# The feed-forward first half with tokens as the stationary operand, 512 weight columns moving, f transposed, and first tokens' products inside the second tokens' norm

## The chip, the cores and the metric

One core of one Trainium2 chip runs the whole program in one launch. The metric is device microseconds (us) of that launch, the median over the runs shown; rows of the trace come from one further, profiled execution. TensorE is called PE in the rows, its weight loads PEld, VectorE DVE, ScalarE ACT, GpSimd POOL, and SyncE, which issues most transfers, SP.

## The reference

Two decoder layers over 256 tokens of width 1024. Each layer is feed-forward, mixer (three attentions and gates), feed-forward; each of these six stages starts with an RMS norm whose scale and shift come from a vector c through the large matrix `w_ada`, and ends by adding a gated result to x.

```python
def swiglu(h, wg, wu, wd):
    return (jax.nn.silu(h @ wg) * (h @ wu)) @ wd
...
for l in range(DEPTH):
    h = pre(x, 0)
    x = x + 0.5 * mod[:, 0, 2] * swiglu(h, w_ffn_gate[l, 0], w_ffn_up[l, 0], w_ffn_down[l, 0])
    h = pre(x, 1)
    ...
    x = x + mod[:, 1, 2] * (merged @ w_out[l])
    h = pre(x, 2)
    x = x + 0.5 * mod[:, 2, 2] * swiglu(h, w_ffn_gate[l, 1], w_ffn_up[l, 1], w_ffn_down[l, 1])
return rmsnorm(x, final_gain)
```

Here `wg` and `wu` are 1024 x 2816 and `wd` is 2816 x 1024, so the inner width is 22 blocks of 128.

## The kernel before, in words

The stages are numbered s = 0 to 5: 0, 2, 3 and 5 are feed-forwards, 1 and 4 are mixers. All instructions stand in the order of the Python code; every engine works through its own queue in that order.

**Units.** Every weight matrix comes through SBUF in raws of 1 MB (three buffers). A raw is cut into units of 128 x 1024 numbers. For each unit `feed` puts a rounded copy `wH` on ScalarE (L150) and the remainder `wL` on VectorE (L158), up to five units ahead of the products, in six buffers each. The activations are split the same way (hH and hL, ffH and ffL), and a matrix product is the sum of three: hH with wH, hH with wL, hL with wH. `step` feeds, takes at most one tick of the `w_ada` work (a multiply-add `acc` on VectorE, L282, over a transfer of 512 KB), issues the unit's products, and then the elementwise work of the unit before (`post`, and a part `later` that comes one unit after it).

**First half of a feed-forward.** `aform` (L595) holds a 128 x 128 block of the weights in TensorE and lets 256 tokens of hH or hL move: 24 products per unit, one inner block fb per unit, gate and up side by side in one PSUM bank. The result stands with the inner width on the partitions, which is what the second half needs: `up_post` makes silu (ScalarE, L653), f = up times silu (VectorE, L654), and then ffH (L657) and ffL (L658).

**Second half and mixer output.** `run_rows` holds 128 x 128 blocks of ffH or ffL, with tokens as columns, and lets 512 columns of `wd` move (`bform`, L707, PSUM names pd and pe).

**From one stage to the next.** The last four units are done for tokens 0 to 127 (t = 0) first and for the second half of the tokens (t = 1) last. So the norm of t = 0 (transposes `psn` at L489, scale and shift at L506 and L508, cast to hH at L520, remainder hL at L526) runs under the last products, and the norm of t = 1 comes after them: residual, square, rsqrt on GpSimd, xn on ScalarE and VectorE, transposes, hH, hL. Three kinds of work may stand in between: `ada_reduce` sums a finished `acc` over the partitions (PE, `adag` at L343 for a gate, `adam` at L352 and L358 for scale or shift), and N1 says how many of the sums stand ahead of the second transposes; before a mixer `v_early` does the products of the first two v units (L943, PSUM pv) for t = 0. Before a feed-forward nothing of that kind is done. A mixer then loads its bias table (L440) through GpSimd's queue and further raws of `w_in` through SP's.

Of the kernel before, what the change touches and what calls it, by code (L numbers as in the profile page):

```python
# [16 lines left out]
P = 128  # L17
# [26 lines left out]

N1 = (0, 1, 2, 2, 1, 0)

# [43 lines left out]
class Trunk:  # L90
# [28 lines left out]
    def load_raws(self):  # L119
        while self.n_raw < min(self.raw_cap, len(self.raws)):  # L120
# [15 lines left out]
            self.n_raw += 1  # L136

    def feed(self, ahead=AHEAD, high=0):

        self.load_raws()  # L140
        nc = self.nc
        lim = min(self.consumed + ahead, self.consumed + NB - 1, len(self.units) - 1)
        while self.n_l <= lim:
            want_h = max(min(self.n_l + 1, lim), self.consumed + high)
            while self.n_h <= want_h:
                u = self.units[self.n_h]
                k, n = u.shape
                th = self.sp.tile([P, 1024], F32R, tag="wH", name=f"wH{self.n_h}", bufs=NB)
                u.H = th[:, : k * n].rearrange("p (k n) -> p k n", k=k)
                nc.scalar.copy(u.H, u.view(self.raw_tiles[u.raw]))  # L150
                self.n_h += 1
# [369 lines left out]

    def norm_low(self, t, h32):
        sl = slice(t * P, (t + 1) * P)
        for q in range(2):
# [45 lines left out]
    def step(self, u):  # L570
# [3 lines left out]
        self.done()  # L574
        if self.pending:
            self.pending()
            self.pending = None
        if u.post:
            self.pending = u.post()

    def flush(self):
        if self.pending:
            self.pending()
            self.pending = None

# [21 lines left out]
    def plan_ffn(self, l, i, s):  # L607
        a = self.a
        wg, wu, wd = a["w_ffn_gate"][l, i], a["w_ffn_up"][l, i], a["w_ffn_down"][l, i]
        plan = {"kind": "ffn", "s": s, "in": [], "out": []}  # L610
        ps = {}

# [23 lines left out]

        def gate_pe(fb):
            def pe(u, part="all"):
                if part != "low":
                    ps[fb] = self.ps(f"pf{s}_{fb}")  # L640
                self.aform(u, ps[fb][:, :S], self.hH, self.hL, part=part)
            return pe

        def up_pe(fb):
            return lambda u: self.aform(u, ps[fb][:, S:], self.hH, self.hL)

        def up_post(fb):
            def post():
                nc = self.nc
                p = ps[fb]  # L650
                sil = self.sil[:, fb % 3, :]
                f32 = self.f32[:, fb % 3, :]
                nc.scalar.activation(sil, p[:, :S], AF.Silu)  # L653
                nc.vector.tensor_tensor(f32, p[:, S:], sil, op=ALU.mult)  # L654

                def later():
                    nc.scalar.copy(self.ffH[:, fb, :], f32)  # L657
                    nc.vector.tensor_tensor(self.ffL[:, fb, :], f32, self.ffH[:, fb, :], op=ALU.subtract)  # L658
                return later
            return post  # L660

        if s == 0:
            plan["start"] = []
            k4 = lambda t, n: t[:, :4 * n].rearrange("p (k n) -> p k n", k=4)
            for q in range(4):
# [11 lines left out]
                plan["start"].append(us)  # L677
        for q in range(3 if s == 0 else 0, NF // 2):
            rg, ru = self.col_raw(wg, ((q * 256, 256),)), self.col_raw(wu, ((q * 256, 256),))
            for r, mk in ((rg, gate_pe), (ru, up_pe)):  # L680
                for b in range(2):
                    fb = 2 * q + b
                    view = lambda t, b=b: t.rearrange("p (k n) -> p k n", k=KB)[:, :, b * P:(b + 1) * P]
                    u = Unit(r, view, (KB, P), mk(fb), up_post(fb) if r == ru else None)
                    self.units.append(u)
                    plan["in"].append(u)
        plan["out"] = self.plan_rows(wd, NF)
# [21 lines left out]
    def run_rows(self, us, s, xh, xl, early=None):  # L709
# [4 lines left out]
        last = s == 5  # L714
        nxt = [ch for ch, at in self.filler.items() if at == s]
        cols = PIECES
# [4 lines left out]
        for kb in range(n - TAIL):  # L721
# [5 lines left out]
            self.done()  # L727
            self.flush()
        for c in LATE:
# [60 lines left out]
    def alloc_ffn(self, s):  # L790
        self.ffH = self.sp.tile([P, NF, S], F32R, tag="bigA", name=f"ffH{s}", bufs=1)
        self.ffL = self.sp.tile([P, NF, S], F32R, tag="bigB", name=f"ffL{s}", bufs=1)
        self.sil = self.sp.tile([P, 3, S], F32, tag="oA", name=f"sil{s}", bufs=1)
        self.f32 = self.sp.tile([P, 3, S], F32, tag="oB", name=f"f32{s}", bufs=1)

    def run_ffn(self, plan, early=None):
# [3 lines left out]
        if s:  # L800
            us = plan["in"][:2]
            for u in us:
                self.feed()
                self.ada_tick()
                u.pe(u, "high")
            for u in us:
                u.pe(u, "low")
            self.done(2)
        for i, u in enumerate(plan["in"]):
            if i > 1 or s == 0:  # L810
# [5 lines left out]
        self.flush()  # L816
        self.run_rows(plan["out"], s, self.ffH, self.ffL, early)
# [117 lines left out]
    def v_pe(self, i, u, pv, ts=(0, 1), part="all"):  # L935
        for t in ts:
            sl = slice(t * P, (t + 1) * P)
            out = pv[t][i // 4][:, (i // 2 % 2) * 256:(i // 2 % 2) * 256 + 256]
            seq = [(self.hH, w, k) for k in range(4) for w in (u.H, u.L)] + [(self.hL, u.H, k) for k in range(4)]
# [6 lines left out]
    def v_early(self, plan):  # L946

        s = plan["s"]
        plan["pv"] = [[self.ps(f"pv{s}_{t}_{i}") for i in range(2)] for t in range(2)]
        for i in range(2):  # L950
            self.v_pe(i, plan["v"][i], plan["pv"], (0,))

    def v_post(self, t, pv):
        self.nc.scalar.copy(self.v[:, t, 0:512], pv[0])
        self.nc.scalar.copy(self.v[:, t, 512:768], pv[1][:, 0:256])

# [181 lines left out]

    def run_mixer(self, plan):
        s, l = plan["s"], plan["l"]  # L1140
# [11 lines left out]
        pv = plan["pv"]  # L1152
        for i, u in enumerate(plan["v"]):
            self.feed()
            self.ada_tick()
            self.v_pe(i, u, pv, (1,) if i < 2 else (0, 1), "high" if i < 2 else "all")
            if i == 1:
                for k in range(2):
                    self.v_pe(k, plan["v"][k], pv, (1,), "low")
                self.done(2)  # L1160
            elif i > 1:
                self.done()
        for t in range(2):
# [25 lines left out]
        for i, u in enumerate(sum(plan["br"], [])):  # L1189
# [4 lines left out]
            for fn, arg in when.get(("br", i), ()):  # L1194
                fn(arg)
        self.flush()
        self.run_rows(plan["out"], s, self.mH, self.mL)

    def run(self):
        nc, a = self.nc, self.a  # L1200
        self.pending = None
        self.ada_setup()
# [97 lines left out]
        for n, plan in enumerate(plans):  # L1300
# [14 lines left out]
            if s == 5:  # L1315
                self.fg = self.sp.tile([P, D], F32, tag="gate", name="fg", bufs=2)
                nc.gpsimd.dma_start(self.fg, a["final_gain"].unsqueeze(0).to_broadcast([P, D]))
            if plan["kind"] == "ffn":
                mix = plans[n + 1] if n + 1 < len(plans) and plans[n + 1]["kind"] == "mix" else None
                self.run_ffn(plan, (lambda: self.v_early(mix)) if mix else None)  # L1320
            else:
                self.run_mixer(plan)

# [28 lines left out]
```

## Time and profile before

| what | value |
|---|---|
| median of 3 runs | 1208.26 us (1208.2 to 1210.25) |
| profiled execution, its own time | 1207.99 us |
| its span in the trace | 1206.3 us |
| granted TensorE clock, mean | 0.998 of full speed |
| busy share PE, DVE, ACT | 98%, 69%, 51% |

The profiled execution is 0.27 us under the median, and 1.7 us of its time lie outside the span. Busy time of PE is the union of instructions whose modelled ends overlap, so the distance from start to start, which the pieces of the chain give as time divided by count, is what one product costs.

### The profile page before, as it was taken

The page shows a single profiled execution, that of the slowest core. Times are in us where ns is not written, and L with a number is a line of the kernel's source. Part 1 is how long each engine was busy: PE and PEld are TensorE (multiplying, and loading weights), DVE is VectorE, ACT ScalarE, POOL GpSimd, SP SyncE. Part 2 cuts the span into 40 slices and gives each one's busy share as a digit, 9 for nine tenths or more (in the row PEclk, how much of TensorE's full clock was granted, in tenths as well). Part 3 has the DMA queues.
Part 4 walks back from the last instruction along what each step waited for, and adds up shares of the span by engine and source line. Part 5 has one row for each costly group of instructions (what it writes and reads, how often), then busy time and mean ns, then how long its engine had stood idle before and what let it go on. Part 6 is the DMA issues. An engine that isn't in the chain of part 4 may idle for free.

```text
span 1206.3 us, 21161 instructions
## 1 busy us (share of the span) xinstructions
PE 1177.2 (98%) x8765; PEld 1099.6 (91%) x8765; DVE 838.2 (69%) x1087; ACT 615.7 (51%) x953; POOL 37.7 (3%) x74
## 2 busy tenths in 40 slices
PE   6999999999999999999999999999999999999997
PEld 5999988899999899998889999889999998999986
DVE  3677776768788797777687676666866788555544
ACT  5555443565564574444364545345655446444432
POOL 1001000300000000000000000012000000000000
PEclk9999999999999999999999999999999999999999
DMA  9999789796658678788849777759853574656550
GB/s 317 310 312 314 268 303 321 127 334 214 209 190 313 213 248 284 264 300 278 294 142 302 265 259 255 271 159 211 292 202 114 177 276 147 204 179 195 177 184 35
DMA packets 190440, 285.35 MB, mean 237 GB/s; under 512 B 8006, under 2 KB 156780, under 8 KB 190344
## 3 DMA queue, kind: packets, MB, share of 16 engines
q1 hardware_dynamic: 187656, 279.88, 69.5%
q0 software_dynamic: 2544, 3.93, 2.6%
q8 instruction: 68, 1.11, 0.4%
q14 instruction: 28, 0.23, 0.1%
q10 hardware_dynamic: 144, 0.20, 0.0%
HBM read 282.77 MB, written 1.20 MB: 235 GB/s over the span
## 4 chain that ended last, share of the span: by engine, by line
PE 87%; DMA 3%; ACT 3%; DVE 3%; issue 2%; POOL 1%; SPq 0%; POOLq 0%; ACTq 0%; DVEq 0%
PE pf L595 39%; PE pd L707 21%; PE pg L595 12%; PE pq L595 3%; PE pb L595 3%; PE pf L625 3%; DMA raw<-in_w_in 2%; DVE wL L158 1%; ACT wH L150 1%; PE adaf L211 1%; DMA first<-in_w_ada 1%; ACT jk L453 1%; ACT h L508 1%; PE pv L943 1%; PE adag L343 0%
## 5 line engine op out<-in xcount | busy, mean ns | idle before, releaser
L158 DVE TENSOR_TENSOR wL<-raw,wH 128x1024 fp32r<-128x1024 f32 (+1 forms) x384 | 462.1, 1212 | 251.2 <-ACT wH L150 250.7
L150 ACT CAST wH<-raw 128x1024 fp32r<-128x1024 f32 (+1 forms) x384 | 394.2, 1041 | 275.5 <-PE pd L707 112.5
L595 PE MATMUL pf<-hH,wH 128*128 128x256 f32 x1312 | 323.9, 285 | 1.1 <-DVE hH L506 1.1
L595 PE MATMUL pf<-hH,wL 128*128 128x256 f32 x1312 | 322.1, 283 | 0.0
L595 PEld LDWEIGHTS pf<-hH,wH 128*128 128x128 f32 x1312 | 251.8, 192 | 4.1 <-DVE hH L506 1.8
L595 PEld LDWEIGHTS pf<-hH,wL 128*128 128x128 f32 x1312 | 252.2, 192 | 0.2 <-issue 0.2
L595 PE MATMUL pf<-hL,wH 128*128 128x256 f32 x1312 | 183.7, 283 | 0.0
L595 PEld LDWEIGHTS pf<-hL,wH 128*128 128x128 f32 x1312 | 169.1, 192 | 0.0
L282 DVE SCALAR_TENSOR_TENSOR acc<-ada,sc,acc 128x1024 f32<-128x1024 f32 x112 | 143.3, 1279 | 5.3 <-DMA ada<-in_w_ada 5.3
L707 PE MATMUL pd<-wH,ffH 128*128 128x512 f32 x336 | 131.3, 391 | 0.0
L707 PE MATMUL pd<-wL,ffH 128*128 128x512 f32 x336 | 130.9, 390 | 0.0
L707 PE MATMUL pd<-wH,ffL 128*128 128x512 f32 x336 | 130.9, 389 | 0.0
L595 PE MATMUL pg<-hH,wH 128*128 128x256 f32 x384 | 96.1, 288 | 0.0
L595 PE MATMUL pg<-hH,wL 128*128 128x256 f32 x384 | 94.0, 283 | 0.0
L653 ACT ACTIVATE sil<-pf 128x256 f32<-128x256 f32 x88 | 33.3, 382 | 108.2 <-PE pf L595 108.2
L595 PEld LDWEIGHTS pg<-hH,wH 128*128 128x128 f32 x384 | 73.4, 191 | 2.7 <-issue 0.9
L707 PEld LDWEIGHTS pd<-wH,ffH 128*128 128x128 f32 x336 | 63.1, 188 | 13.7 <-issue 0.8
L707 PEld LDWEIGHTS pd<-wH,ffL 128*128 128x128 f32 x336 | 63.1, 188 | 13.1
L707 PEld LDWEIGHTS pd<-wL,ffH 128*128 128x128 f32 x336 | 63.1, 188 | 12.8
L595 PEld LDWEIGHTS pg<-hH,wL 128*128 128x128 f32 x384 | 73.6, 192 | 0.0
L654 DVE TENSOR_TENSOR f<-pf,sil 128x256 f32<-128x256 f32 x88 | 36.9, 422 | 34.0 <-ACT sil L653 34.0
L595 PE MATMUL pq<-hH,wH 128*128 128x256 f32 x224 | 56.1, 288 | 0.0
(214 smaller groups left out, 1456.0 us busy)
## 6 DMA issues: line engine op xcount, KB each, us to landing
ada<-in_w_ada SPq DMA_DIRECT2D x128, 512.0 KB, 5.4
raw<-in_w_ffn_down SPq DMA_DIRECT2D x44, 1024.0 KB, 5.1
raw<-in_w_in SPq DMA_DIRECT2D x42, 1024.0 KB, 6.7
raw<-in_w_ffn_gate SPq DMA_DIRECT2D x41, 1024.0 KB, 5.9
raw<-in_w_ffn_up SPq DMA_DIRECT2D x41, 1024.0 KB, 5.5
first<-in_w_ada SPq DMA_DIRECT2D x32, 256.0 KB, 6.0
raw<-in_w_out SPq DMA_DIRECT2D x8, 1024.0 KB, 5.8
raw<-in_w_ffn_gate SPq DMA_DIRECT2D x12, 256.0 KB, 6.0
```

The source lines that it names most:

```text
L150: nc.scalar.copy(u.H, u.view(self.raw_tiles[u.raw]))
L158: nc.vector.tensor_tensor(u.L, u.view(self.raw_tiles[u.raw]), u.H, op=ALU.subtract)
L211: self.nc.tensor.matmul(self.first_ps[q % 2][32 * i:32 * i + 32, 0:P], w, src[:, i * P:(i + 1) * P], start=kb in (0, None), stop=kb == KB - 1)
L282: self.nc.vector.scalar_tensor_tensor(acc, src, sc, acc, ALU.mult, ALU.add)
L453: nc.scalar.activation(junk[:, :w], self.x[:, t, lo:lo + w], AF.Square, scale=1.0 / 32.0, accum_out=ms[:, n:n + 1])
L508: nc.scalar.activation(out[:, fb, :], src, AF.Identity, bias=sb, scale=sa)
L595: nc.tensor.matmul(out, w[:, kb, cs], x[:, kb, :], start=i == 0, stop=i == n - 1)
L625: self.nc.tensor.matmul(ps[fb][:, S * up:S * up + S], w[:, 2 * k + up, b * P:(b + 1) * P], x[:, 2 * q + k, :], start=q == 0 and not up and ...
L653: nc.scalar.activation(sil, p[:, :S], AF.Silu)
L654: nc.vector.tensor_tensor(f32, p[:, S:], sil, op=ALU.mult)
L707: self.nc.tensor.matmul(out, x[:, kb, sl], w[:, 0, hs], start=first and i == 0, stop=last and i == 2)
L943: self.nc.tensor.matmul(out, x[:, 4 * (i % 2) + k, sl], w[:, k, :], start=i % 2 == 0 and j == 0, stop=i % 2 == 1 and j == n - 1)
```

## The change

The first half of the feed-forward turns round: a 128 x 128 block of hH or hL (tokens as columns) is held, and 512 columns of `wg` or `wu` move (`cols_pe`). The inner width is done in groups of four blocks (and a last group of two, with 256 columns); a group has four units of gate and four of up, a unit being two k blocks by 512 columns. The result stands with tokens on the partitions, so f is transposed: `cols_post` makes f for a group, and its `later`, one unit after that, issues four transposes per token half (`pft`) and takes ffH and ffL from PSUM. In stage 0 the first six blocks keep the old form. hH and hL become two halves of one tile.

At a stage's end every next stage now has an early part (`ffn_early`, `v_early`): the products of the next stage's first units for t = 0 stand ahead of the second transposes, and one `ada_reduce` fewer does (N1). The second half of hL of t = 0 is made after xn, the third unit's wH is fed before the second transposes and its wL between hH and h32 of t = 1, and the first units' products with hL of t = 1 come last. `flush` at the end of each row loop becomes `drain`, which takes posts one unit later.

```diff
-N1 = (0, 1, 2, 2, 1, 0)
+N1 = (0, 0, 1, 1, 0, 0)
...
             evac(self.hH[:, :, sl])
             for f in between:
                 f()
+            self.feed(2)
         evac(h32)
...
-        self.hH = self.sp.tile([P, KB, S], F32R, tag="hH", name=f"hH{s}", bufs=1)
-        self.hL = self.sp.tile([P, KB, S], F32R, tag="hL", name=f"hL{s}", bufs=1)
+        self.hHL = self.sp.tile([P, KB, 2, S], F32R, tag="hHL", name=f"hHL{s}", bufs=1)
+        self.hH, self.hL = self.hHL[:, :, 0, :], self.hHL[:, :, 1, :]
...
         if u.post:
-            self.pending = u.post()
+            self.pending.append(u.post)
+
+    def drain(self):
+
+        todo, self.pending = self.pending, []
+        for f in todo:
+            later = f()
+            if callable(later):
+                self.pending.append(later)
...
+        def cols_pe(g, up, k0, nk, n):
+
+            def pe(u, ts=(0, 1), part="all"):
+                for t in ts:
+                    if k0 == 0 and part != "low":
+                        pg[g, up, t] = self.ps(f"pf{s}_{g}_{up}_{t}")
+                    out = pg[g, up, t][:, :n]
+                    sl = slice(t * P, (t + 1) * P)
+                    seq = [(self.hH, w, k) for k in range(nk) for w in (u.H, u.L)]
+                    seq += [(self.hL, u.H, k) for k in range(nk)]
+                    for i in {"all": range(3 * nk), "high": range(2 * nk), "low": range(2 * nk, 3 * nk)}[part]:
+                        x, w, k = seq[i]
+                        self.nc.tensor.matmul(out, x[:, k0 + k, sl], w[:, k, :], start=k0 == 0 and i == 0,
+                                              stop=k0 + nk == KB and i == 3 * nk - 1)
+            return pe
...
+        def cols_post(g, n):
+
+            def post():
+                nc = self.nc
+                f = wide(self.f32, n)
+                for t in range(2):
+                    nc.vector.tensor_tensor(f[:, t, :], pg[g, 1, t][:, :n], wide(self.sil, n)[:, t, :], op=ALU.mult)
+
+                def later():
+                    b = n // P
+                    for t in range(2):
+                        pt = self.ps(f"pft{s}_{g}_{t}")
+                        for i in range(b):
+                            nc.tensor.transpose(pt[:, i * P:(i + 1) * P], f[:, t, i * P:(i + 1) * P], self.ident)
+                        src = pt[:, :n].rearrange("p (b n) -> p b n", b=b)
+                        sl = slice(t * P, (t + 1) * P)
+                        H, L = self.ffH[:, g:g + b, sl], self.ffL[:, g:g + b, sl]
+                        nc.scalar.copy(H, src)
+                        nc.vector.tensor_tensor(L, src, H, op=ALU.subtract)
                 return later
             return post
...
-        if early:
-            self.norm_low(0, h0)
-            early()
+        self.norm_low(0, h0, (0,))
+        early()
         xn1 = self.norm_x(1, s + 1)
-        if not early:
-            self.norm_low(0, h0)
+        self.feed_high(self.consumed + 2)
+        self.norm_low(0, h0, (1,))
...
+            us = plan["in"][:3]
+            for u in us[:2]:
+                self.ada_tick()
+                u.pe(u, (1,), "high")
+            self.ada_tick()
+            us[2].pe(us[2], (0,))
+            us[2].pe(us[2], (1,), "high")
             for u in us:
+                u.pe(u, (1,), "low")
+                self.done()
                 self.feed()
```

How the change moves instructions is seen at three places. First TensorE's queue from the mixer's last product (pe) of stage 1 to the first products of stage 2 (pf); wH and wL are weights, psn the norm's transposes of the second tokens, adag a filler sum. Before:

```order
L707 MATMUL pe_768_4487<-wH_4452,mHL_4025 128x256
L343 MATMUL adag_0_4615<-acc_2_3915,ones 128x512
L343 MATMUL adag_1_4616<-acc_2_3915,ones 128x512
L489 MATMUL psn_1_0_4627<-ident,xn_1_4622 128x128 x4
L489 MATMUL psn_1_1_4632<-ident,xn_1_4622 128x128 x4
L595 MATMUL pf_0_4682<-hH_4574,wH_4470 128x256
```

And of the change: the twelve products of units 0 and 1 for the first tokens begin right behind the last pe, and these rows are the last three of them and what follows.

```order
L672 MATMUL pf_0_0_0_4237<-wH_4110,hHL_4196 128x512
L672 MATMUL pf_0_0_0_4237<-wL_4112,hHL_4196 128x512
L672 MATMUL pf_0_0_0_4237<-wH_4110,hHL_4196 128x512 x2
L491 MATMUL psn_1_0_4259<-ident,xn_1_4253 128x128 x4
L491 MATMUL psn_1_1_4264<-ident,xn_1_4253 128x128 x4
L345 MATMUL adag_0_4269<-acc_2_3535,ones 128x512
L345 MATMUL adag_1_4270<-acc_2_3535,ones 128x512
L672 MATMUL pf_0_0_1_4316<-wH_4092,hHL_4196 128x512
```

The first tokens' products have taken the place of the sum adag, which now stands between the second tokens' transposes and their first products. Second, TensorE's queue of the change around the transposes (pft) of stage 2's first group; the products ahead of them are those of the next group's second unit, the products behind them those of its third.

```order
L672 MATMUL pf_4_0_1_4465<-wL_4376,hHL_4196 128x512
L672 MATMUL pf_4_0_1_4465<-wH_4374,hHL_4196 128x512 x2
L698 MATMUL pft_0_0_4493<-ident,f_4315 128x128 x4
L698 MATMUL pft_0_1_4500<-ident,f_4315 128x128 x4
L672 MATMUL pf_4_0_0_4458<-wH_4396,hHL_4196 128x512
```

Two units of products (24) stand between the end of a group and its transposes. Third, VectorE's queue of the change at the same place: f is the product of up and silu, and the wL ahead of it belongs to the unit that is fed just before.

```order
L284 SCALAR_TENSOR_TENSOR acc_0_4321<-ada_4360,sc,acc_0_4321 128x1024
L160 TENSOR_TENSOR wL_4454<-raw_4351,wH_4452 128x1024
L691 TENSOR_TENSOR f_4315<-pf_0_1_0_4380,sil_4314 128x512
L691 TENSOR_TENSOR f_4315<-pf_0_1_1_4387,sil_4314 128x512
L160 TENSOR_TENSOR wL_4476<-raw_4378,wH_4474 128x1024
L284 SCALAR_TENSOR_TENSOR acc_0_4321<-ada_4401,sc,acc_0_4321 128x1024
L703 TENSOR_TENSOR ffL_4313<-pft_0_0_4493,ffH_4312 128x4x128
L703 TENSOR_TENSOR ffL_4313<-pft_0_1_4500,ffH_4312 128x4x128
```

Where four pairs of f and ffL of 256 columns stood one by one between the wL, two of 512 stand together now, and the ffL wait for transposes.

## Rows read from the trace of the kernel before

**Rows 1.** The page's head and its busy times: us, share of the span, instructions

```profile
span 1206.3 us, 21161 instructions
...
PE 1177.2 (98%) x8765; PEld 1099.6 (91%) x8765; DVE 838.2 (69%) x1087; ACT 615.7 (51%) x953; POOL 37.7 (3%) x74
```

**Rows 2.** The page's chain that ended last, by engine and line

```profile
PE pf L595 39%; PE pd L707 21%; PE pg L595 12%; PE pq L595 3%; PE pb L595 3%; PE pf L625 3%; DMA raw<-in_w_in 2%; DVE wL L158 1%; ACT wH L150 1%; PE adaf L211 1%; DMA first<-in_w_ada 1%; ACT jk L453 1%; ACT h L508 1%; PE pv L943 1%; PE adag L343 0%
```

**Rows 3.** Windows, stage 2's first half: us, busy us (count), clock, DMA share, GB/s

```profile
425.00:553.00 128.00, 128.00 (x1071) 126.89 (x1071) 98.18 (x120) 67.66 (x100) 0.00 (x0) 1.00 0.83 279
```

**Rows 4.** The chain's pieces in order of time: start us, us, what, count

```profile
60.84 48.96 PE pf L595 x408
...
318.22 0.98 PE pt_dil L1109 x9
...
806.18 1.09 PE psn L489 x8
...
808.35 1.72 PE adag L343 x4
...
1011.61 127.21 PE pf L595 x1056
...
1138.82 54.44 PE pd L707 x240
```

**Rows 5.** Groups by form: count | busy us, mean ns of one | idle before, releaser

```profile
L158 DVE TENSOR_TENSOR wL<-raw,wH 128x1024 fp32r<-128x1024 f32 x372 | 452.0, 1223 | 244.3 <-ACT wH L150 243.8
...
L150 ACT CAST wH<-raw 128x1024 fp32r<-128x1024 f32 x372 | 385.4, 1050 | 272.7 <-PE pd L707 112.5 <-PE pf L595 73.4 <-issue 29.9
...
L282 DVE SCALAR_TENSOR_TENSOR acc<-ada,sc,acc 128x1024 f32<-128x1024 f32 x112 | 143.3, 1279 | 5.3 <-DMA ada<-in_w_ada 5.3
...
L536 DVE SCALAR_TENSOR_TENSOR y<-pd,gate 128x512 f32<-128x512 f32 x24 | 16.5, 688 | 14.8 <-PE pd L707 14.8
...
L506 DVE TENSOR_SCALAR h<-psn,modv 128x128 f32<-128x128 f32 x40 | 13.6, 403 | 0.0
```

**Rows 6.** Timeline, PE, stage 1 to 2: start, us, [idle before <-releaser]

```profile
419.34 1.88 PE L343 MATMUL adag<-acc,ones 128*128 128x512 f32 x4
...
422.63 1.09 PE L489 MATMUL psn<-ident,xn 128*128 128x128 f32 x8 [1.41 <-DVE xn L478]
...
424.15 0.39 PE L595 MATMUL pf<-hH,wH 128*128 128x256 f32 x1 [0.43 <-DVE hH L506]
```

**Rows 7.** Timeline, ACT and DVE, same place

```profile
420.15 0.62 ACT L520 CAST hH<-h 128x512 fp32r<-128x512 f32 x1
...
422.09 0.49 DVE L478 TENSOR_SCALAR xn<-x,r 128x512 f32<-128x512 f32 x1 [0.66 <-POOL r L468]
```

**Rows 8.** Timeline, PE, stage 2 to 3

```profile
617.53 1.09 PE L489 MATMUL psn<-ident,xn 128*128 128x128 f32 x8 [0.85 <-DVE xn L478]
...
619.05 0.39 PE L595 MATMUL pf<-hH,wH 128*128 128x256 f32 x1 [0.21 <-DVE hH L506]
```

**Rows 9.** Timeline, PE, stage 0 to 1

```profile
218.58 0.28 PE L707 MATMUL pe<-wH,ffL 128*128 128x256 f32 x1
...
220.16 0.39 PE L943 MATMUL pv<-wH,hH 128*128 128x256 f32 x1 [1.30 <-ACT hH L520]
...
229.37 0.39 PE L943 MATMUL pv<-wL,hH 128*128 128x256 f32 x1 [0.62 <-DVE wL L158]
...
247.24 0.39 PE L595 MATMUL pq<-hH,wL 128*128 128x256 f32 x1 [0.34 <-DVE wL L158]
```

**Rows 10.** Timeline, PE, stage 3 to 4

```profile
817.67 1.36 PE L943 MATMUL pv<-wH,hL 128*128 128x256 f32 x8 [0.62 <-DVE hL L526]
...
819.75 0.39 PE L943 MATMUL pv<-wL,hH 128*128 128x256 f32 x1 [0.61 <-DVE wL L158]
```

**Rows 11.** The chain's pieces, transfers behind the two mixers' starts

```profile
230.48 14.29 DMA raw<-in_w_in
...
820.86 13.75 DMA raw<-in_w_in
```

More of the change, by code (lines that the diff above doesn't have):

```diff
@@ L136, in load_raws, with feed_high @@
             self.n_raw += 1
+    def feed_high(self, want):
+        while self.n_h <= want:
+            u = self.units[self.n_h]
+            k, n = u.shape
+            th = self.sp.tile([P, 1024], F32R, tag="wH", name=f"wH{self.n_h}", bufs=NB)
+            u.H = th[:, : k * n].rearrange("p (k n) -> p k n", k=k)
+            self.nc.scalar.copy(u.H, u.view(self.raw_tiles[u.raw]))
+            self.n_h += 1
     def feed(self, ahead=AHEAD, high=0):
@@ L143, in feed @@
         while self.n_l <= lim:
[L144 to L151, printed above, removed]
+            self.feed_high(max(min(self.n_l + 1, lim), self.consumed + high))
             if self.n_l >= self.n_h:
@@ L520, in norm_high, with norm_low @@
         self.nc.scalar.copy(self.hH[:, fs, sl], h32[:, fs, :])
-    def norm_low(self, t, h32):
+    def norm_low(self, t, h32, qs=(0, 1)):
         sl = slice(t * P, (t + 1) * P)
-        for q in range(2):
+        for q in qs:
             fs = slice(4 * q, 4 * q + 4)
@@ L677, in plan_ffn @@
                 plan["start"].append(us)
[L678 to L686, printed above, removed]
+        g = 6 if s == 0 else 0
+        while g < NF:
+            b = min(4, NF - g)
+            n, nk = b * P, 1024 // (b * P)
+            kl = 2048 // n
+            for up, w in ((0, wg), (1, wu)):
+                for h in range(KB // kl):
+                    r = self.add_raw([(lambda t, kl=kl: t.rearrange("p (k n) -> p k n", k=kl),
+                                       w[P * kl * h:P * kl * h + P * kl, g * P:g * P + n]
+                                       .rearrange("(k p) n -> p k n", p=P))])
+                    for i in range(2):
+                        k0 = kl * h + nk * i
+                        post = None
+                        if k0 + nk == KB:
+                            post = (cols_post if up else gate_post)(g, n)
+                        u = Unit(r, lambda t, kl=kl, nk=nk, i=i: t.rearrange("p (k n) -> p k n", k=kl)[:, nk * i:nk * i + nk, :],
+                                 (nk, n), cols_pe(g, up, k0, nk, n), post)
+                        self.units.append(u)
+                        plan["in"].append(u)
+            g += b
         plan["out"] = self.plan_rows(wd, NF)
@@ L949, in v_early @@
         plan["pv"] = [[self.ps(f"pv{s}_{t}_{i}") for i in range(2)] for t in range(2)]
-        for i in range(2):
-            self.v_pe(i, plan["v"][i], plan["pv"], (0,))
+        for i, part in enumerate(("all", "high")):
+            self.v_pe(i, plan["v"][i], plan["pv"], (0,), part)
     def v_post(self, t, pv):
-        self.nc.scalar.copy(self.v[:, t, 0:512], pv[0])
-        self.nc.scalar.copy(self.v[:, t, 512:768], pv[1][:, 0:256])
+        v = self.v[:, t, :].rearrange("p (b n) -> p b n", b=3)
+        self.nc.scalar.copy(v[:, 0:3:2, :], pv[0].rearrange("p (b n) -> p b n", b=2))
+        self.nc.scalar.copy(v[:, 1, :], pv[1][:, 0:256])
     def sb_stages(self, s):
@@ L1137, in soft_stages, with run_mixer @@
         return s1, s1e, s1b, s2, s3
[L1139 removed]
+    def run_mixer(self, plan, early):
         s, l = plan["s"], plan["l"]
@@ L1152, in run_mixer @@
         pv = plan["pv"]
-        for i, u in enumerate(plan["v"]):
+        vs = plan["v"]
+        self.v_pe(1, vs[1], pv, (0,), "low")
+        for i in range(2):
+            self.ada_tick()
+            self.v_pe(i, vs[i], pv, (1,), "high")
+        self.ada_tick()
+        self.v_pe(2, vs[2], pv, (0,))
+        self.v_pe(2, vs[2], pv, (1,), "high")
+        for i in range(3):
+            self.v_pe(i, vs[i], pv, (1,), "low")
+            self.done()
+            self.feed()
+        for i in range(3, len(vs)):
             self.feed()
             self.ada_tick()
[L1156 to L1162, printed above, removed]
+            self.v_pe(i, vs[i], pv)
+            self.done()
         for t in range(2):
@@ L1317, in run @@
                 nc.gpsimd.dma_start(self.fg, a["final_gain"].unsqueeze(0).to_broadcast([P, D]))
+            after = plans[n + 1] if n + 1 < len(plans) else None
+            early = None
+            if after:
+                early = lambda: (self.ffn_early if after["kind"] == "ffn" else self.v_early)(after)
             if plan["kind"] == "ffn":
[L1319 to L1320 removed]
+                self.run_ffn(plan, early)
             else:
[L1322 removed]
+                self.run_mixer(plan, early)
 _INS = ["x", "c", "w_ada", "b_ada", "norm_gain", "w_ffn_gate", "w_ffn_up", "w_ffn_down", "w_in", "w_br_sb", "w_br_dil",
```

60 lines of the change are left out of this document (27 added, 33 removed).

## The prediction, made before the change was run

> **What bounds the kernel now.** I read the page's head first: PE is busy for 1177.2 of 1206.3 us, DVE for 69%, ACT for 51% [rows 1]. Since a busy PE is a union of overlapping ends, the chain that ended last comes next: it runs through PE, and the first half of the feed-forwards (`pf`, L595) is 39% of it, the second half (`pd`) 21% [rows 2]. In stage 2's first half PE has no gap at all, while DVE is busy for 98 of 128 us, ACT for 68, and the DMA engines for 0.83 of their time, at a granted clock of 1.00 [rows 3]. So a product less, or a cheaper one, counts in full there. The pieces of the chain give the price: 1056 products of 256 columns take 127.21 us, 120.5 ns each, and 240 products of 512 columns take 54.44 us, 226.8 ns each [rows 4]. The other place where time can be won is the start of each stage, where PE does stand: 1.41 and 0.43 us at the start of stage 2 [rows 6], 0.85 and 0.21 at stage 3 [rows 8], 1.30, 0.62 and others at stage 1 [rows 9], 0.62 and 0.61 at stage 4 [rows 10].
>
> **The turned first half.** From 120.5 and 226.8 ns a column costs (226.8 - 120.5) / 256 = 0.415 ns, and each product has a fixed part of 120.5 - 256 x 0.415 = 14.2 ns beside its columns. The change keeps the columns and halves the instructions. In stages 2, 3 and 5 the 1056 products (22 blocks, gate and up, 24 each) become 480 of 512 columns and, for the last two blocks, 96 of 256: 480 x 226.8 + 96 x 120.5 ns = 120.4 us, 6.8 us less than 127.2. In stage 0 sixteen blocks change: 768 x 120.5 = 92.5 us (the 408 that stand together there took 120.0 each [rows 4]) become 384 x 226.8 = 87.1, 5.4 less. Sum: 3 x 6.8 + 5.4 = 25.8 us saved by 1824 fewer instructions. That a held block of activations with 512 weight columns moving costs 226.8 is not an assumption about another kind of product: `pd` holds ffH and moves `wd` in just this way.
>
> A rule speaks against this. The Trainium skill ("TensorE: Matmul & The Clock Gate", section "Back-to-back issue gap") gives a warm gap of N / 2.4 + 2.5 ns. By it the 1824 instructions would be worth only 4.6 us, and the estimate for the whole would be about 1220 us, slower than before. The trace has 14.2 ns where the page has 2.5, in 1296 products of two loops, and I go by the trace.
>
> **The transposes added.** f must be turned: 22 blocks times two token halves are 44 transposes in stages 2, 3 and 5, 32 in stage 0, 164 in all, in 22 bursts, 19 of eight and, for the last two blocks of three stages, 3 of four. Nine transposes between products cost the mixer 0.98 us, 109 ns each; eight `psn` between products of the row loop held the chain for 1.09 us, with the return to products in it [rows 4]. The lower bound is 164 x 0.109 = 17.9 us, the upper 164 / 8 x 1.09 = 22.3. I take the middle, 20.1, since the `pt` bursts are the nearer case and the second figure holds a step back that they also pay in part. The first half is then worth 25.8 - 20.1 = 5.7 us (3.5 to 7.9): most of the gain is spent on PE itself.
>
> **Do the transposes wait?** They stand two units behind the end of their group, 24 x 0.227 = 5.44 us. In that time VectorE must reach f: the unit's wH on ACT 1.05, its wL 1.22, at most one `acc` 1.28 [rows 5], and two f of 512 columns from PSUM, for which the nearest row is y at 0.69 [rows 5]: 4.93 us. The margin is 0.5 us, and 1.2 for the first four transposes. Before, nothing on PE waited that closely for DVE. The cover is that DVE keeps no backlog: it stood 244 us waiting for ACT's wH [rows 5]. I put 0.5 us in the sum for single late bursts, most likely in stage 0, 1 at most in the range. ACT and DVE otherwise do the same elements in fewer instructions, and wait for the transposes only behind five units of prepared weights (13 us), so this costs nothing; without those units it would be about a microsecond per group. Transfers: the same megabytes at a pace higher by (6.8 - 5.4) / 127, 1%, against a DMA share of 0.83: nothing.
>
> **The starts of stages 2, 3 and 5.** At the start of stage 2 PE goes from 419.34 to 424.15, 4.81 us, and does `adag` (1.72 us by [rows 4]) and eight transposes (0.89) in it: 2.2 us lost [rows 6]. Now the twelve early products come first. They need the first half of hH, which ACT casts at 420.15 for about 0.6 us [rows 7], so PE stands some 1.46 us, as before stage 1's `pv` today (218.58 + 0.12 to 220.16 [rows 9]). They end at about 420.8 + 12 x 0.227 = 423.5, and xn is ready at 422.6 [rows 7] (the half of hL put ahead of it falls into DVE's 0.66 us and more of waiting), so the transposes follow at once; `adag`, moved behind them, covers the 1.36 us (13.6 / 10 [rows 5]) of hH of the second tokens. The late products with hL are reached 1.72 + 18 x 0.227 = 5.8 us after the transposes, against hH 1.36, wL 1.22, h 1.36 and two hL 1.4 on DVE, 5.3 us. New loss 1.46 and a little; gain 0.7 to 1.0 where `adag` alone stands there (stages 2 and 5), I take 0.9 each. At stage 3 two sums stood ahead and covered more, 0.85 + 0.21 us idle remain [rows 8]; now one short sum of them does: gain 0.7. Together 2.5 us, with 1.5 and 3.2 as bounds since each wait was read to some tenths only.
>
> **The starts of the mixers.** The waits for hL (0.62) and wL (0.61) [rows 9, 10] should go, since the third unit's weights come earlier and the products with hL last: with the restart behind each that is some 1.5 us at both; at stage 4 the sum that covered the first wait has moved, which takes part of it back. But behind both starts the chain passes through a raw of `w_in` that takes 14.29 and 13.75 us to land [rows 11], while the bias table is loaded too, and at stage 1 PE waits again at 247.24 [rows 9]. If that landing stays where it is, the gain waits there; if it moves with its issue (the wL that frees the buffer comes 0.6 to 1.4 us earlier), that much is kept. Bounds 0 to 0.9 and 0 to 1.4; I take 0.5 and 0.7, 1.2 us.
>
> **Sum.** 5.7 + 2.5 + 1.2 - 0.5 = 8.9 us less: 1207.99 becomes 1199.1 in the profiled execution's terms, and 1208.26 - 8.9 = 1199.4 as a median. Best ends: 7.9 + 3.2 + 2.3 = 13.4, 1194.9. Worst ends: 3.5 + 1.5 + 0 - 1.0 = 4.0, 1204.3.
>
> **Rivals.** First, absorbed: transposes at their upper price, and the starts return nothing because the transfers behind them or the norm's own chain set the time. Gain 3.5 less 1: 1204.8 to 1205.8, and with a little more stall no change that shows. For it: rows 11 and the wait at 247.24; against it: two of the three feed-forward starts have no transfer in their chain.
>
> Second, slower: f comes late. If DVE does one more `acc` ahead of f, or an `acc` waits for its transfer (5.3 us of such waits in all [rows 5]), f ends 1.28 us later and PE stands 1.28 - 0.5 = 0.8 us in each burst: 22 x 0.8 = 17.6 us, less 9.4 without the stall term, 1216.5. It decides from 9.4 / 22 = 0.43 us per burst. Against it: DVE's idle time, and one tick per unit at most in most units.
>
> Third, also slower: the fixed part stays with the columns in the new loop, so that 512 columns cost two times 120.5. Then nothing is saved, 20.1 us of transposes are added and 3.2 won: 1225. `pd` speaks against it. This is what the skill's rule of 2.5 ns would come near to.
>
> **Chances.** My forecast with its bounds 0.75, absorbed 0.11, late f 0.09, no saving per product 0.03, more than 13.4 us gained 0.02. A measurement of this kernel can tell about 0.2%, 2.4 us, from no change. Faster by more than that: 0.75 + 0.02 and the better half of the absorbed case, 0.82; same: the rest of it and mild stalls, 0.09; slower 0.09. The range 1194.9 to 1206.0 holds the forecast and the better part of the absorbed case, about 0.81; the forecast's own is 1194.9 to 1204.3.
>
> **What would show it.** Right: 512-column `pf` at 227 ns start to start; stage 2's first half with its transposes about 126 us where 127.2 were; bursts of eight `pft` in about 1 us without idle time ahead of them; at the start of stage 2 one wait of about 1.3 us for hH and none ahead of `psn`; a wait of PE near 247 that grows at stage 1. Wrong: idle time ahead of `pft` released by DVE's f in most groups, products of 240 ns, or starts whose waits reappear at the products with hL.

## The result and the profile after

The changed kernel takes 1201.86 us (median of 4 runs, 1199.14 to 1203.11), the kernel before 1208.87 beside it: ratio 0.9935, 95% interval 0.9921 to 0.9949. The forecast was 1199.4, its range 1194.9 to 1206.0. The profiled execution took 1201.48 us with a span of 1199.7, 6.6 less than before.

The head of the page and its chain by line, as in [rows 1, 2]:

```profile
PE 1172.9 (98%) x7105; PEld 1023.3 (85%) x7105; DVE 830.7 (69%) x1011; ACT 607.4 (51%) x877; POOL 37.8 (3%) x74
...
PE 84%; DMA 5%; DVE 4%; ACT 4%; issue 2%; POOL 1%; SPq 0%; POOLq 0%; ACTq 0%; DVEq 0%
PE pf L672 35%; PE pd L763 21%; PE pg L603 12%; PE pq L603 4%; PE pb L603 3%; DMA raw<-in_w_in 2%; PE pf L633 2%; PE pft L698 2%; DVE wL L160 1%; DMA ada<-in_w_ada 1%; PE adag L345 1%; ACT wH L144 1%; ACT jk L455 1%; DVE acc L284 1%; ACT h L510 1%
```

`pf` has gone from 39% of the chain to 35%, and 2% of it came back as `pft`. The waits of PE in the whole program (total us, times, longest):

```profile
PE pf L672 <- ACT hHL L523: 3.4, 3, 1.3
...
PE pv L1006 <- ACT hHL L523: 2.1, 2, 1.3
PE pq L603 <- DVE wL L160: 1.8, 2, 0.9
...
PE po L1073 <- ACT z L1064: 1.1, 1, 1.1
PE pq L603 <- ACT wH L144: 1.0, 1, 1.0
```

The waits for xn and hL of [rows 6, 8, 9, 10] are gone. In their place stand one wait for the first tokens' hH at each of five starts (stage 1's stood there before, 1.30 us [rows 9]), and longer waits of `pq` in the mixers. To see what each part is worth I read from the timeline where the first product of each phase starts, and take the differences: pe is the first product of a row loop's last four units, pd the first of a row loop, pq and pg the first of q/k and of the gates (us).

| stretch | before | changed | |
|---|---|---|---|
| span's start to pe of stage 0 | 214.72 | 213.62 | -1.10 |
| stage 1, pe to pq (its start and v) | 26.15 | 23.79 | -2.36 |
| stage 1, pq to pg | 50.54 | 53.34 | +2.80 |
| stages 2, 3, 5: pe to pd | 137.76, 136.80, 135.83 | 135.13, 134.24, 133.11 | -2.63, -2.56, -2.72 |
| stages 2, 3, 5: pd to next pe | 57.15 each | 57.64 each | +0.49 each |
| stage 4, pe to pq | 27.03 | 25.63 | -1.40 |
| stage 4, pq to pg | 49.32 | 51.17 | +1.85 |

All other stretches are equal to 0.05 us, and the 0.49 are the last group's transposes, which now stand behind pd. Of stage 0's 1.10 us, 0.90 were gained from the loop's first product on. Each of the other feed-forwards gained 2.07 to 2.23 us, the forecast's 2.1 to 2.3. The mixers lost 0.44 and 0.45 where 0.5 and 0.7 were to be gained: 2.1 of the 2.3 us between the forecast's sum, 8.9, and the span's 6.6 lie there, and so the experiments begin there. The chain in the changed kernel's stage 1 (start, us, what), as [rows 11]:

```profile
228.47 14.64 DMA raw<-in_w_in
...
243.21 1.05 ACT wH L144
244.26 0.02 issue
244.29 1.24 DVE wL L160
245.53 0.04 issue
245.57 7.40 PE pq L603 x47
```

The raw is issued 2.01 us earlier than before and lands 1.67 us earlier. But PE reaches q/k 3.45 us earlier than before, so the wait foreseen near 247 grew. PE's timeline and the windows (busy us of PE, PEld, DVE, ACT, POOL, granted clock, DMA share, GB/s) there:

```profile
244.31 0.38 PE L603 MATMUL pq<-hHL,wH 128*128 128x256 f32 x1 [0.98 <-ACT wH L144]
...
245.57 0.38 PE L603 MATMUL pq<-hHL,wL 128*128 128x256 f32 x1 [0.88 <-DVE wL L160]
...
246.61 0.41 PE L603 MATMUL pq<-hHL,wL 128*128 128x256 f32 x1
...
246.82 0.41 PE L603 MATMUL pq<-hHL,wH 128*128 128x256 f32 x1
```

```profile
223.00:243.00 20.00, 20.00 (x168) 19.98 (x167) 11.15 (x15) 7.28 (x13) 7.58 (x14) 1.00 1.07 140
243.00:246.00 3.00, 1.14 (x7) 0.74 (x6) 1.71 (x2) 1.99 (x2) 0.00 (x0) 1.00 1.09 359
246.00:250.00 4.00, 4.00 (x23) 4.00 (x22) 4.00 (x4) 3.44 (x6) 0.00 (x0) 0.57 1.07 362
```

Behind the two waits the granted clock falls: products stand 0.21 us apart where 0.12 is usual, the 1.2 GHz level, and the window's mean is 0.57. It holds 23 products where 33 would fit at 0.12 us, by that estimate another 1.2 us that no wait shows. And from 223 to 243 us the DMA engines are full but move only 140 GB/s; the bias table's 16 loads lie there.

### The profile page after: what moved, and what is told of

It is laid out like the page before. It is cut to its first block, busy times and chain, and to the rows that moved or that the text cites. A ratio compares the mean times of both kernels' runs of the same rounds, so it can differ in the third digit from the quotient of the medians.

```text
span 1199.7 us, 17743 instructions
## 1 busy us (share of the span) xinstructions
PE 1172.9 (98%) x7105; PEld 1023.3 (85%) x7105; DVE 830.7 (69%) x1011; ACT 607.4 (51%) x877; POOL 37.8 (3%) x74
## 4 chain that ended last, share of the span: by engine, by line
PE 84%; DMA 5%; DVE 4%; ACT 4%; issue 2%; POOL 1%; SPq 0%; POOLq 0%; ACTq 0%; DVEq 0%
PE pf L672 35%; PE pd L763 21%; PE pg L603 12%; PE pq L603 4%; PE pb L603 3%; DMA raw<-in_w_in 2%; PE pf L633 2%; PE pft L698 2%; DVE wL L160 1%; DMA ada<-in_w_ada 1%; PE adag L345 1%; ACT wH L144 1%; ACT jk L455 1%; DVE acc L284 1%; ACT h L510 1%
## 5 line engine op out<-in xcount | busy, mean ns | idle before, releaser
L672 PE MATMUL pf<-wH,hHL 128*128 128x512 f32 (+1 forms) x1408 | 418.5, 378 | 3.4 <-ACT hHL L523 3.4
L672 PEld LDWEIGHTS pf<-wH,hHL 128*128 128x128 f32 x1408 | 258.6, 188 | 53.8 <-ACT hHL L523 4.3
L672 PE MATMUL pf<-wL,hHL 128*128 128x512 f32 (+1 forms) x704 | 260.9, 375 | 0.0
L672 PEld LDWEIGHTS pf<-wL,hHL 128*128 128x128 f32 x704 | 132.6, 188 | 23.7 <-issue 0.7
L603 PE MATMUL pg<-hHL,wH 128*128 128x256 f32 x768 | 145.4, 285 | 0.0
L603 PEld LDWEIGHTS pg<-hHL,wH 128*128 128x128 f32 x768 | 121.8, 192 | 2.7 <-issue 0.9
L603 PE MATMUL pg<-hHL,wL 128*128 128x256 f32 x384 | 94.0, 283 | 0.0
L603 PE MATMUL pq<-hHL,wH 128*128 128x256 f32 x448 | 85.4, 289 | 1.0 <-ACT wH L144 1.0
L763 PEld LDWEIGHTS pd<-wL,ffH 128*128 128x128 f32 x336 | 63.1, 188 | 12.8
L603 PEld LDWEIGHTS pq<-hHL,wH 128*128 128x128 f32 x448 | 71.8, 195 | 2.0 <-ACT wH L144 1.2
L603 PEld LDWEIGHTS pg<-hHL,wL 128*128 128x128 f32 x384 | 73.4, 191 | 0.0
```

Of the source, the lines that this page charges most:

```text
L603: nc.tensor.matmul(out, w[:, kb, cs], x[:, kb, :], start=i == 0, stop=i == n - 1)
L672: self.nc.tensor.matmul(out, x[:, k0 + k, sl], w[:, k, :], start=k0 == 0 and i == 0, stop=k0 + nk == KB and i == 3 * nk - 1)
L763: self.nc.tensor.matmul(out, x[:, kb, sl], w[:, 0, hs], start=first and i == 0, stop=last and i == 2)
```

## The experiments

Times are medians; each ratio is to the kernel before, run on the same chip in the same job. The first four rows are of one job, the next four of a second and the last four of a third, each on its own chip, and the kernel before had medians of 1208.96, 1210.82 and 1210.12 us there. So a difference of a microsecond or two between rows of different jobs proves little by itself, and the stretches decide.

| kernel | us | ratio, 95% interval |
|---|---|---|
| mixers' start as before | 1202.26 | 0.9939, 0.9926 to 0.9951 |
| table's loads later in the code | 1203.12 | 0.9945, 0.9933 to 0.9958 |
| no table loaded | 1199.39 | 0.9918, 0.9905 to 0.9932 |
| feed-forward starts as before | 1203.52 | 0.9948, 0.9935 to 0.9962 |
| table on SP's queue | 1195.08 | 0.9877, 0.9863 to 0.9892 |
| the same, mixers' start as before | 1198.76 | 0.9908, 0.9893 to 0.9922 |
| transposes twice | 1219.60 | 1.0076, 1.0059 to 1.0093 |
| 256 columns | 1228.16 | 1.0150, 1.0135 to 1.0165 |
| before, with the table on SP's queue | 1207.21 | 0.9973, 0.9963 to 0.9983 |
| table on SP's queue, feed-forward starts as before | 1195.49 | 0.9883, 0.9868 to 0.9897 |
| table on SP's queue, sums first | 1191.81 | 0.9855, 0.9837 to 0.9872 |
| transposes one unit earlier | 1225.31 | 1.0129, 1.0110 to 1.0149 |

### The mixers' start alone undone

```diff
-        for i, part in enumerate(("all", "high")):
-            self.v_pe(i, plan["v"][i], plan["pv"], (0,), part)
+        for i in range(2):
+            self.v_pe(i, plan["v"][i], plan["pv"], (0,))
```

The loop over the v units, the place of hL and N1 of stage 3 go back with it.

> The feed-forwards stay as changed; only the two mixers start as before the change (both v units whole for the first tokens, hL whole ahead of them, the third unit's weights not fed early, at stage 4 two sums ahead of the second transposes). Theory: the raw of w_in that lands together with the bias table sets when the mixer goes on, so the changed start returns nothing and its earlier arrival is paid back with waits and with a stretch of half clock: 0.5 to 2 us faster than the changed kernel (1201.9), 1200 to 1201.4. Rival: the changed start is worth the 1.2 us forecast, and something else in the stages lost 2 us: 1203.

1202.26 lies between the two and alone settles nothing. The stretches do: pe to pq takes 26.17 and 27.03 us, as before the change, so the changed start is worth 2.4 and 1.4 us where it stands; pq to pg takes 51.44 and 50.16, 1.9 and 1.0 less than in the changed kernel's profiled run. Most of the gain is paid back behind it.

### The table's loads later in the code, and no table

```diff
-        self.load_bias(self.T)
...
+            if 2 <= i < 10:
+                self.load_bias(self.T, 16 * (i - 2), 2)
```

> The 16 loads of the bias table are issued two at a time behind units 2 to 9 of q and k, where all 16 stood at the mixer's beginning. Theory: these loads crowd the raws of w_in; without them the raws land in well under 14 us, PE does not wait between 243 and 246 us nor near 831, the clock does not fall, and 3 to 5 us are won on the changed kernel: 1197 to 1199. Rival: the raws are late by themselves (issue and share of the w_ada transfers), or the spread loads crowd the next raws as much: 1201 to 1203.

This tested nothing. GpSimd's timeline shows the first loads (start, us):

```profile
221.74 5.88 POOL L442 DMA_DIRECT2D Tm<-scr  x10 [0.70 <-issue]
```

That is where they began before (221.20 in the changed kernel). GpSimd's queue held nothing else between its part of the second tokens' norm and these loads, and they began 0.7 us behind it in both kernels, so the later place in the code did not hold them back; it is the changed kernel once more, at 1203.12.

```diff
-        self.load_bias(self.T)
...
+                nc.gpsimd.memset(self.T, 0.0)
```

> The bias table is not loaded at all: its tile is filled with zeros on GpSimd behind unit 4 of q and k, so the softmax heads get no bias and no mask. Theory (table crowds the raws): at least what spreading the loads wins, 4 to 6 us less than the changed kernel, 1196 to 1198, and no wait of PE between 243 and 246 us. Rival (raws late by themselves): waits stay, 1201 to 1202.

1199.39, 2.5 us less than the changed kernel and 1.4 short of the theory's nearer end, although PE waits for no weights in the mixers any more. The shortfall is of the experiment's own making: the fill ran ahead too, beside VectorE's xn. Two rows, of VectorE and of GpSimd:

```profile
221.04 2.85 DVE L480 TENSOR_SCALAR xn<-x,r 128x512 f32<-128x512 f32 x1 [0.66 <-POOL r L470]
```

```profile
220.96 2.66 POOL L1255 MEMSET Tm<- 128x3072 f32 x1
```

The same xn takes 0.49 us in the changed kernel. PE waited 1.7 us for it at both mixers.

### The feed-forwards' starts alone undone

```diff
-        self.norm_low(0, h0, (0,))
-        early()
+        mix = s in (0, 3)
+        if mix:
+            self.norm_low(0, h0, (0,))
+            early()
         xn1 = self.norm_x(1, s + 1)
```

`run_ffn` begins with two units for both token halves again, and N1 puts the sums ahead of the second transposes as before.

> Only the feed-forwards' starts go back to the order before the change: no early products of the first tokens, the sums ahead of the second transposes as before, hL behind xn. Theory: 0.9 + 0.7 + 0.9 us come back as loss, 1204.4. Rival: early products only move the wait from the transposes to the first product and are worth nothing: 1202; or more than forecast, since stage 2, 3 and 5 gained 2.1 to 2.2 us each and the turned half might have given less than its 1.4 to 1.6: 1206.

The median, 1203.52, seems to bear out a part of the 2.5 us, but the trace does not. Pe to pd takes 135.12, 134.33 and 133.11 us in stages 2, 3 and 5, the changed kernel's own to 0.1. What is slower lies in stage 1, whose code is the same in both; here the raw took 16.72 us to land (14.64 in the changed kernel's profiled run). PE's waits and the window:

```profile
247.13 0.58 PE L604 MATMUL pq<-hHL,wH 128*128 128x256 f32 x1 [3.07 <-ACT wH L144]
248.39 0.58 PE L604 MATMUL pq<-hHL,wL 128*128 128x256 f32 x1 [0.68 <-DVE wL L160]
```

```profile
246.00:254.00 8.00, 6.19 (x29) 5.90 (x30) 6.89 (x6) 6.56 (x9) 0.00 (x0) 0.57 1.04 346
```

So the landing varies from run to run by some 2 us, and the half clock adds to it: pq to pg of stage 1 took 53.3 to 56.2 us in the six profiled runs with this start and GpSimd's loads.

### The table on SP's queue, with either start

```diff
-            self.nc.gpsimd.dma_start(T[r:r + 8], src)
+            self.nc.sync.dma_start(self.T[r:r + 8, 6 * h:6 * h + 6], src)
...
+            if 4 <= i < 12:
+                self.load_bias(0, 2 * (i - 4), 2)
...
+            if 1 <= i < 5:
+                self.load_bias(1, 4 * (i - 1), 4)
```

> The bias table is loaded through SP's queue, behind the raws of w_in, in two halves by heads: the first six heads two loads at a time behind units 4 to 11 of q and k, the other six four at a time behind units 1 to 4 of the branches. GpSimd's queue, which waits for no other engine, loaded it at the mixer's beginning even where the code stood later. Theory (the table crowds the raws): the raws of w_in land in about 8 us, PE does not wait near 243 to 249 us nor near 831, the clock stays up there, and 3 to 5 us are won on the changed kernel: 1197 to 1199. Rival: the spread loads crowd the raws behind them as much: 1201 to 1203.

> The bias table moved as in the run beside this one, and the two mixers start as before the change. Theory: once the table is out of the way, the changed start of the mixers is worth what was forecast for it, so this is 1.0 to 1.5 us slower than the run beside it: 1198 to 1200.5. Rival: the changed start is worth nothing by itself, whatever lands behind it: equal within 0.4 us.

1195.08: 6.8 us off the changed kernel, more than the theory asked; pq to pg is 3.9 and 2.8 us shorter. From the second tokens' norm on, the chain of stage 1 stays on PE, and the window from 223 to 243 us has 222 GB/s at a DMA share of 0.66:

```profile
222.47 0.87 PE psn L491 x8
223.34 14.97 PE pv L1006 x124
238.31 11.52 PE pq L603 x96
```

```profile
223.00:243.00 20.00, 20.00 (x169) 19.98 (x167) 18.03 (x23) 13.15 (x21) 0.00 (x0) 1.00 0.66 222
```

With the old start 1198.76, 3.7 us more, where 1.0 to 1.5 were forecast: the changed start is worth 2.37 us in stage 1 and 1.42 in stage 4, and all of it shows once nothing behind it is late. The Trainium skill ("DMA: Bandwidth & Descriptors", section "Issuing engines are not separate DMA queues") says that transfers from all engines run on the same sixteen and interleave; the raws' slow landing beside GpSimd's loads agrees. That the loads are what crowds the raws is also shown by the kernel without them, whose pq to pg takes the same 49.45 and 48.34 us. Whether the other queue or the later time helped was not separated.

### The kernel before, with the table on SP's queue

> The kernel before the change, with nothing new but the bias table through SP's queue in two halves. Theory: before the change the raws of w_in were late only by tenths (0.3 and 0.6 us of waits of PE, and the restarts), so the table costs it little: 0.5 to 1.5 us faster than before, 1207.4 to 1208.4 by the 1208.9 of the first runs; the change is then worth 12 to 13 us where the table is out of the way. Rival: the table slows more than PE's waits show (all transfers behind it, the products' clock): 3 us or more faster, 1206 or less.

1207.21; by the ratio 2.1 to 4.5 us less than before, where the theory had 0.5 to 1.5. The stretches say 2.1: pq to pg went from 50.54 and 49.32 to 49.45 and 48.33 us. All five kernels with the table on SP's queue have the same there to 0.01, so the crowded raws cost 1.1 and 1.0 us before the change, and 3.9 and 2.8 in the changed kernel's profiled run (3.9 to 6.7 and 2.2 to 3.6 in the six profiled runs with its start and GpSimd's loads). With the table out of the way the change is worth 10 to 12 us: the profiled spans went from 1204.1 to 1193.9, the medians, from two jobs, from 1207.2 to 1195.1.

### The early products and the sums, with the table out of the way

> The table through SP's queue (1195.1 with the change whole), and the feed-forwards' starts as before the change. From the last product of one stage to the first of the row loop of the next, the earlier run without the early products took 135.1, 134.3 and 133.1 us in stages 2, 3 and 5, the changed kernel the same. Theory by that: the early products are worth nothing, 1195.1 within 0.4. By the forecast 2.5 us slower: 1197.6.

1195.49 against 1195.08, from two jobs; pe to pd differs by 0.09, 0.08 and 0.17 us. So early products with the sums behind them are worth no more than no early products with the sums in front, to some 0.2 us.

```diff
-N1 = (0, 0, 1, 1, 0, 0)
+N1 = (0, 1, 2, 2, 1, 0)
```

> The table through SP's queue, and the sums of w_ada ahead of the early products as before the change, where they would cover the wait for the first tokens' hH (1.1 to 1.3 us per feed-forward start). If the start is set by the norm's chain on the other engines, the wait moves behind the second transposes and nothing is won: 1195.1 within 0.5. If the wait was loss of its own, 1 us is won at each of three or four starts: 1191.5 to 1192.5.

1191.81, 3.3 us faster by the medians and 3.4 by the stretches, and the fastest of all. So the wait was loss of its own. PE's rows at the start of stage 2, first of the changed kernel, then with the sums first:

```profile
420.18 0.50 PE L672 MATMUL pf<-wH,hHL 128*128 128x512 f32 x1 [1.33 <-ACT hHL L523]
...
423.08 1.03 PE L491 MATMUL psn<-ident,xn 128*128 128x128 f32 x8
...
423.95 1.88 PE L345 MATMUL adag<-acc,ones 128*128 128x512 f32 x4
...
425.27 0.79 PE L672 MATMUL pf<-wH,hHL 128*128 128x512 f32 x1
425.90 0.40 PE L672 MATMUL pf<-wL,hHL 128*128 128x512 f32 x1
```

```profile
414.71 1.88 PE L345 MATMUL adag<-acc,ones 128*128 128x512 f32 x4
...
416.20 0.62 PE L672 MATMUL pf<-wH,hHL 128*128 128x512 f32 x1
...
419.21 1.04 PE L491 MATMUL psn<-ident,xn 128*128 128x128 f32 x8
...
420.31 0.50 PE L672 MATMUL pf<-wH,hHL 128*128 128x512 f32 x1
```

The sum ahead covers the wait for hH. Behind the transposes next to nothing needs cover: products follow 1.10 us after the first of them, where the transposes alone take 0.87, since the late products begin with the first feature blocks of hH and do not need all eight. Pe to pd fell by 1.07, 0.50 and 0.95 us in stages 2, 3 and 5, and pe to pq of stage 4 by 0.84. Against the kernel without early products, which also has its sums in front, pe to pd is 0.98, 0.58 and 1.12 us shorter: that, 2.7 us, is what the early products themselves can give.

### What products and transposes cost

> Every burst of transposes of f is issued twice, the second over the first; the output is the same. It measures what a transpose costs apart from the return to products. By the changed kernel's rows (0.099 us from transpose to transpose) 164 more cost 16.2 us: 1218. By the price in the forecast's sum (0.1225 each) 20.1: 1222.

```diff
-                        for i in range(b):
+                        for i in [*range(b), *range(b)]:
```

1219.6, 17.7 more, 108 ns each, between the two and nearer the first. Stages 2, 3 and 5, where PE waits for no raw, grew by 4.8 to 4.9 us for 44 transposes each, 109 to 111 ns. Sixteen took 1.75 us in the chain (start, us, what), eight in the changed kernel 0.87:

```profile
456.60 1.75 PE pft L698 x16
```

```profile
425.83 24.53 PE pf L672 x108
450.37 0.87 PE pft L698 x8
```

> Groups of two blocks, so that 256 weight columns move instead of 512 (only the first group of stages 2, 3 and 5 keeps 512): the same columns in 1536 more products, and 16 more bursts of transposes of half the length. If each product has a fixed part of 14.2 ns, 21.8 us are added, and the 16 more returns at about 0.1 us make 1.6: 1225. If the fixed part were 2.5 ns, 3.8 and 1.6: 1207.

```diff
-            b = min(4, NF - g)
+            b = 4 if s and g == 0 else 2
```

1228.16, 26.3 more. Stages 2, 3 and 5 are undisturbed: pe to pd grew by 4.74, 4.91 and 4.83 us for 384 products more, 12.3 to 12.8 ns each. The pieces say the same:

```profile
500.62 11.51 PE pf L672 x96
512.12 0.44 PE pft L698 x4
```

256 columns take 119.9 ns, 512 take 24.53 / 108 = 227.1, and two of the one less one of the other leave 12.7. The rest is stage 0, 11.6 us more: 384 products at 12.7 ns make 4.9, one late f made PE wait 4.5, and the granted clock has a mean of 0.89 between 60 and 90 us.

### The transposes one unit earlier

```diff
-                return later
+                later()
```

> The transposes of f stand one unit (2.72 us) earlier, straight behind the instructions that make f. By the changed kernel's trace the first half of f is ready 1.1 to 2.6 us ahead of them and the second 0.6 later, so PE would wait 0.3 to 1.8 us at each of 22 bursts, about 15 us in all: 1217. By the forecast's margin of 0.5 us it would be 2.2 us each: 1250. No loss at all would say that f is ready far earlier.

1225.31, 23.4 more. The waits are what the trace promised, not the 48 us of the forecast's margin:

```profile
PE pft L698 <- DVE f L691: 14.1, 19, 2.9
```

For the other 9 us the trace offers the slower first products behind 19 waits and a clock mean of 0.97 between 60 and 110 us; how much each of them took was not separated.

## Why the prediction held, point by point

**The turned half** was right: columns cost the same held either way round. 512 of them cost 227.1 ns here and 226.8 in `pd` before. By the pieces of the 256-column kernel the fixed part is 12.7 ns, not 14.2, so 1824 fewer products are worth 23.2 us, not 25.8; the transposes cost the lower bound, 164 x 0.109 = 17.9, not 20.1. 5.3 us remain where 5.7 were forecast: two errors of over 2 us each cancel, which was luck. The rival that the fixed part stays with the columns would have 2 x 119.9 ns for 512 columns, and fell too. The forecast took N / 2.4 + 2.5 ns for the page's rule of a stream of products. The Trainium skill ("TensorE: Matmul & The Clock Gate", section "Back-to-back issue gap") gives it for an isolated product, and says that in a stream it counts too much at 512 columns. The trace does not agree: an estimate by the formula is 215.8 ns for 512 columns, where 227.1 were measured, and with 2.5 ns as the fixed part an estimate for the 256-column kernel is 5 us more, where 26 were measured.

**f in time** was right: f's first half ends 1.1 to 2.6 us before the transposes in 21 of 22 bursts, where 1.2 was worked out; the first burst of stage 0 came 0.06 us behind f, and PE stood 0.14 us in it. The slower rival has its place, one unit further on.

**The starts of the feed-forwards** were right in size and wrong in cause. In stage 2, from pe to the products behind the second norm, PE took 8.77 us before and 7.83 now, without the twelve early products' 2.72: 0.94 gained where 0.9 stood in the sum. The first rows of pe, before and now:

```profile
415.38 0.28 PE L707 MATMUL pe<-wH,mHL 128*128 128x256 f32 x1
```

```profile
414.72 0.28 PE L763 MATMUL pe<-wH,mHL 128*128 128x256 f32 x1
```

The first product behind the norm is followed by the next only after 0.63 us (425.27 to 425.90). So the same stretch measured to the 25th product, where the pace has settled, less the products done by then at 120.4 and 226.8 ns each, is the better figure: stages 2, 3 and 5 gained 0.82, 0.66 and 0.88 us, 2.4 where 2.5 were forecast. But the kernel with no early products gained the same to 0.02. Its first product behind the transposes has no wait for hH, which was 0.43 us before [rows 6], because the turned loop begins with the first tokens. So it was luck that the term fitted: the turned loop alone gives this, and the early products give 2.7 us more only if the sums stay in front. The step that failed is "`adag`, moved behind them, covers the 1.36 us ... of hH of the second tokens". It can cover 0.2 us there, and it left the wait for the first hH [rows 7], 1.33 us, bare in front. The forecast had this wait in its sum, at 1.46 us, but took it for the price of the early products; keeping N1 as before the change would have saved it, 3.3 us over four starts, a mixer's among them.

**The starts of the mixers** are the term that was mis-sized: 1.2 us gained in the sum, bounds 0 and 2.3, and 0.9 lost. The mechanism was named, "If that landing stays where it is, the gain waits there", and the raw did land late. Two things were left out of the bounds. The landing varies from run to run (14.64 to 16.91 us in the six profiled runs), and took 0.35 us longer even in the changed kernel's own. And a wait of PE cost more than itself where the half clock followed it. What was there to be gained was larger too: 3.8 us at both starts where the text had some 1.5.

The rival "absorbed" thus came true for the mixers. The early products of the feed-forwards returned nothing either, but not because the norm's chain sets the time: with the sums in front they did.

## What to carry to other kernels

When a start gets earlier, look at what lands next: here 3.8 us of gain turned into a loss of 0.9 until one other transfer was moved, and the whole change was then worth 10 to 12 us instead of 7. Filler work was worth more here in front of the first wait of a chain than behind the last; ask of the last one how much of the tile its first reader needs. A load on a queue that waits for no other engine may start earlier than its place in the code suggests: here moving it later changed nothing (221.74 us against 221.20).

## What was not expected of the hardware

- PE's clock fell to the 1.2 GHz level within a program of 98% busy PE: after waits of 0.98 and 0.88 us (mean 0.57 from 246 to 250 us), and of 3.07 and 0.68 (0.57 from 246 to 254). After waits of 0.6 and 0.9 us, with the mixers' start as before, it stayed at 1.00.
- A GpSimd fill of 2.66 us made VectorE's 128x512 scaling take 2.85 us where it takes 0.49, at both mixers. The Trainium skill ("SBUF — State Buffer", section "Who interferes with whom") says that VectorE's 2-port modes contend with GpSimd, and that whoever issues first has the shared pair of ports for the whole instruction; the two rows agree, with the fill 0.08 us ahead.
- The runs of each changed kernel with the table on SP's queue lie within 0.8 to 1.4 us of each other, those with GpSimd's loads within 1.2 to 4.4. The kernel before with the table on SP's queue spans 2.6, so the table is not the only source of spread.
